# A hybrid decoder step on one core: the recurrence's products on the whole array, and the causal mask set by GpSimd selections

## The chip, the cores and the metric

The kernel runs on one core of one Trainium2 chip. A core has TensorE (PE in the profile; its weight loads are shown apart as PEld), VectorE (DVE), ScalarE (ACT), GpSimd (POOL) and SyncE (SP), which issues nearly all DMAs here. The engines work side by side, each through its own queue in a fixed order, and wait for one another by semaphores. The metric is the device time of one execution in microseconds (us). The time before is the median of three runs, 2099.18 us (2098.11 to 2101.88). A measurement of this kernel can tell a difference of about 0.2% from none.

## What is computed

One decoder layer with two groups of heads. From a prompt of 2048 positions and 64 sample positions, RMSNorm and one input projection give both groups; their gated outputs go through one output projection, a residual and a last norm. Group A is stick-breaking attention, causal over 2048 keys; group B is a matrix recurrence (RWKV-7), which the kernel works in chunks of 64 positions.

```python
def _sb_attend(q, k, v, q_pos, k_pos, sb_bias):
    z = jnp.einsum('bqhd,bkhd->bhqk', q, k) * (HEAD_DIM ** -0.5)
    z = z + sb_bias[None, :, None, None]
    mask = (k_pos[None, :] < q_pos[:, None])[None, None]
    log_keep = jnp.where(mask, jax.nn.log_sigmoid(-z), 0.0)
    between = lax.cumsum(log_keep, axis=3, reverse=True) - log_keep
    a = jnp.where(mask, jnp.exp(jax.nn.log_sigmoid(z) + between), 0.0)
    return jnp.einsum('bhqk,bkhd->bqhd', a, v)

def step(S, inp):                      # _wkv_scan, one position
    r_t, w_t, k_t, v_t, a_t, b_t = inp
    sa = jnp.einsum('bhvk,bhk->bhv', S, a_t)
    S = S * w_t[:, :, None, :] + sa[..., None] * b_t[:, :, None, :] + v_t[..., None] * k_t[:, :, None, :]
    return S, jnp.einsum('bhvk,bhk->bhv', S, r_t)
```

## The kernel before

**Planned order.** Every operation is first recorded (`Plan.op`) with an engine, a cost, what it reads and writes, and a priority. `Plan.issue` then lays them out by a list schedule: each engine takes the ready operation of lowest priority number, and the instructions are emitted in that order, which the chip keeps. TensorE's costs carry a mode: R for products on the whole 128x128 array, T for transposes, A, B, C and E for products on a part of it. `SWITCH` adds a cost when the mode changes. Because all operations are emitted through one helper, the profile gives nearly all of them the line L63; tiles tell them apart, and their buffer numbers are left out there.

**Stage 1 (proj).** The prompt goes in four quarters of 512 positions (`ORDER`, one string for each). `project` multiplies the normed input (`xh`, `xl`: high and low part) by the weights (`wp`): 4056 products of 128x512 or smaller. They have the last priority of all (1e6), so they fill whatever PE time the rest leaves. `rw_unit` handles two heads of the recurrence for one quarter: there are 16 units. `attend` handles two heads of attention for one block of 512 queries.

**A step of the recurrence (`seq`).** A unit has 8 chunks, worked one after another, so 128 steps in all. Each step has four groups of products. `fx` multiplies `L` by `VV` (in the trace `bank<-VV,L`); `fu` multiplies the inverse `NN` by `XT` (`bank<-XT,NN`); `fs` gives the new state from `BKT` and `VV` (`bank<-VV,BKT`); `fy` gives the output (`bank<-L,VV`, `bank<-AR,SZ`, `bank<-RS,VV`). Between them DVE and ACT copy the results from the banks. In `fx`, `fs` and `fy` the two heads use 64 columns of the array each, and `fu` uses 64 columns; so all four are column-tiled (mode A), where the projections use all 128 columns. A product of two f32 operands is two MATMULs in the trace, the xh and wp products (fp32r) are one.

**A chain of attention (`softmax_chain`).** For 128 queries of one head and up to 512 keys: two products of `kt` and `qt` into a bank; ACT computes |z| into `T` and relu(z) into `D`, then exp and ln on `T`; DVE scans `T` and `D` along the keys, then forms z minus the scan into `T`; PE transposes `T` (up to four 128x128); ACT takes the exponential into `At`; PE multiplies `At` by `vt` for two heads at a time (64 columns each). Of 320 such chains 128 are diagonal: their last 128 keys are those of the queries themselves. There a third product, `neg` by `idb` in bf16, adds -30000 where the key is not before the query. There are two `T` and two `D` buffers (more for the last `attend`) and two banks for scores (`ZB`), so two chains are under way at a time. GpSimd copies the carry (`car`) from one key block to the next, and serves the recurrence (`SW`, `SZ`).

**Stage 2.** After the last projection the remaining chains run, with the samples' attention and the output products (`woh`, `wol` by `orw`) beside them; the output products of the last quarter come after the last chain.

Of the kernel before, what the change touches and what calls it, by code (L numbers as in the profile page):

```python
# [79 lines left out]
class Plan:  # L80
# [67 lines left out]
    SWITCH = {("T", "T"): 81.0}  # L148
    for _a in "RT":
        for _b, _x, _y in (("A", 97.0, 55.0), ("B", 97.0, 50.0), ("C", 97.0, 90.0), ("E", 97.0, 15.0)):  # L150
            SWITCH[_a, _b] = _x + 75.0 * (_a == "T")
            SWITCH[_b, _a] = _y
    for _a in "ABCE":
        for _b in "ABCE":
            if _a != _b:
                SWITCH[_a, _b] = 75.0

# [185 lines left out]
class Kern:  # L343
# [146 lines left out]
    def stage1(self, ctx):  # L490
# [36 lines left out]
        self.consts2a()  # L527
# [17 lines left out]
    def consts1(self, S):  # L545
# [29 lines left out]
        bo, mask, mask8 = self.bo, self.mask, self.mask8  # L575
# [20 lines left out]
        op("POOL", 9500, masks, (), ["C1"])  # L596
        op("DVE", 130, lambda: nc.vector.tensor_copy(self.bor, bo), ["C1"], ["C1"])
# [9 lines left out]
        op("DVE", 210, lambda: nc.vector.tensor_copy(shT, bs.t[:, 0:136].rearrange("p (c b) -> p c b", b=8)), [bs.k], ["C1"])  # L607
# [5 lines left out]
    def const_tiles(self, S):  # L613
        nc = self.nc
        for nm, n in (("vt", 64), ("omu", 17), ("oka", 4), ("gneps", 1), ("bo", 128), ("mask", 128), ("mask8", 128), ("pv", 17), ("seqm", 8), ("sbb", 8)):
# [18 lines left out]

        self.d_w = self.tc.dram_tile([33, 2, 128, 1024], F32, name="d_w")
        self.d_x = self.tc.dram_tile([T, 1024], F32, name="d_x")
        self.d_g = self.tc.dram_tile([512, T], F32, name="d_g")

        self.d_o = self.tc.dram_tile([2, 1024, T], F32, name="d_o")

    def attention_tiles(self, S):
# [5 lines left out]
        self.neg = S.tile([128, 128], BF16, "neg")  # L647
        self.idb = S.tile([128, 128], BF16, "idb")
# [178 lines left out]
    def evac_rw(self, hf, ti, t0, Np, Ns, c0, ct, kind, j, bk):  # L827
# [17 lines left out]
        if Np < N:  # L845
# [3 lines left out]
            self.stt(vs[:, :, 0], self.shT[:, ct, :], mu, vs[:, :, 0], ALU.mult, ALU.add, r=[], w=zk, prio=-1)  # L849
# [16 lines left out]
    def rwkv_tiles(self, S):  # L866
# [34 lines left out]
        self.SZ = S.ring(2, [128, 64], F32, "SZ")  # L901
# [246 lines left out]
    def seq(self, hf, j, c, un):  # L1148
# [37 lines left out]
        self.act(xt.t[hi, 1], bx.t[hi, 0:64], AF.Copy, r=[bx.k], w=[(xt.k, 1)], ps=True, prio=-0.5)  # L1186
        bu = self.bank("XB")
        self.pe(224, lambda: self.mm(bu.t[lo, 0:128], un.NN[:, c, :], xt.t.rearrange("p h x -> p (h x)"), True, True), r=nks + [(xt.k, 0), (xt.k, 1)], w=[bu.k], prio=-0.5, mode="A")
        self.copy(VV[lo, s_, 1, 0, :], bu.t[lo, 0:64], r=[bu.k], w=[ku + (0,)], prio=-0.5)
        self.act(VV[lo, s_, 1, 1, :], bu.t[lo, 64:128], AF.Copy, r=[bu.k], w=[ku + (1,)], ps=True, prio=-0.5)  # L1190
        kus = [ku + (0,), ku + (1,)]
        bs = self.bank("XB")
        def fs():
            for h in range(2):
                self.mm(bs.t[hr[h], 0:64], BKT[:, s_, h, :], VV[:, s_, 1, h, :], True, True)
        self.pe(215, fs, r=[kb, kv] + kus, w=[bs.k], prio=-0.5, mode="A")
        last = c == 7
# [4 lines left out]
        if c == 0:
            self.yb = self.bank("YB")
        yb = self.yb
        y0 = 64 * c
        def fy():
            for h in range(2):
                self.mm(yb.t[hr[h], y0:y0 + 64], VV[:, s_, 1, h, :], un.L[h][:, c, 64:128], True, False)
            for h in range(2):
                st, rt = (VV[:, s_, 0, 1, :], un.RS[:, c, :]) if h else (sz.t, un.AR[:, c, 64:128])  # L1210
                self.mm(yb.t[hr[h], y0:y0 + 64], st, rt, False, True)
        self.pe(330, fy, r=kus + [kv, ks, sz.k, ("AR", U, c), ("RS", U)] + lks, w=[yb.k], mode="A")
# [301 lines left out]
    def consts2a(self):  # L1514
        nc = self.nc
        idt = self.ident.t
        neg, idb = self.neg.t, self.idb.t
        def f():
            nc.gpsimd.tensor_copy(idb, idt)

            nc.gpsimd.memset(neg, 0.0)
            nc.gpsimd.affine_select(out=neg, in_=neg, pattern=[[-1, 128]], base=-1, channel_multiplier=1, compare_op=ALU.is_ge, fill=-30000.0)
        self.pool(7800, f, w=["idb", "neg"])

# [51 lines left out]
    def softmax_chain(self, zb, n, bias, bk, car, first, last, rings):  # L1576
# [8 lines left out]
        self.act(t, t, AF.Ln, r=[T.k], w=[T.k], bias=1.0, tab=LNE)  # L1585
        init = 0.0 if first else car[0]
# [9 lines left out]
        self.stt(t, z, bias, d, ALU.add, ALU.subtract, r=[zb.k, D.k], w=[T.k])  # L1596
        return T

    def attend(self, t, j):
# [18 lines left out]
        for kb in range(t, -1, -1):  # L1618
# [6 lines left out]
            for qs in qss:  # L1625
# [3 lines left out]
                for h in range(2):  # L1629
# [6 lines left out]
                    D = self.softmax_chain(zb, n, self.sbb[:, 2 * j + h:2 * j + h + 1], [], (self.car.t[:, c:c + 1], (self.car.k, c)), diag, kb == 0, (self.Tr, self.Dr))  # L1636
# [215 lines left out]
```

## Time and profile before

| | us |
|---|---|
| median of three runs | 2099.18 |
| the profiled execution | 2096.49 |
| its span, first to last instruction | 2094.8 |
| PE busy | 1993.0 (95%), 15130 MATMULs |
| PEld busy | 1497.9 (72%) |
| DVE busy | 1607.3 (77%) |
| ACT busy | 1483.3 (71%) |
| POOL busy | 313.9 (15%), 854 instructions |
| DMA | 380.85 MB, 182 GB/s |

TensorE's clock was granted at 0.986 of its full 2.4 GHz over the span. A matmul's end is modelled and matmuls overlap, so PE's busy share says that something was always under way, not what each product cost. What a group of products costs is read from the starts of the products around it.

### The profile page before, as it was taken

The numbers are of one execution on the slowest core, as the hardware profiler recorded it, in microseconds if no ns is written. First come the engines' busy times: TensorE is split into PE (matmuls) and PEld (weight loads), VectorE is DVE, ScalarE is ACT, GpSimd is POOL, SyncE is SP. The second block draws the span as 40 slices with busy tenths as digits, with TensorE's granted clock in tenths as the row PEclk, the third lists the DMA queues.
The fourth block names the chain that finished last, engine by engine and source line by source line (L and its number), as shares of the span: only waits on it lengthen the run. The fifth ranks groups of instructions, "written<-read, shape, count | busy, mean of one in ns | idle before, by whom it ended". The sixth has DMA issues, their size and how long they took to land. (4 is left out here: it accounts for less than half of the span.)

```text
span 2094.8 us, 43112 instructions
## 1 busy us (share of the span) xinstructions
PE 1993.0 (95%) x15130; PEld 1497.9 (72%) x15130; DVE 1607.3 (77%) x3770; ACT 1483.3 (71%) x3115; POOL 313.9 (15%) x854
## 2 busy tenths in 40 slices
PE   6889999999999999999999999999997999999988
PEld 5787887767777777777677777767675767676645
DVE  7798698665887888788888989889866767676732
ACT  6555454586768787877777876777687888898831
POOL 4122222110012112111221121121112000000000
PEclk9899999999999999999999999999998999999999
DMA  6977746747775675666456555555665656656454
GB/s 232 330 250 213 221 131 196 199 144 238 206 217 148 196 194 150 173 193 179 136 162 184 153 145 145 177 146 159 185 165 160 209 174 187 190 168 178 142 163 132
DMA packets 346551, 380.85 MB, mean 182 GB/s; under 512 B 127923, under 2 KB 247273, under 8 KB 346333
## 3 DMA queue, kind: packets, MB, share of 16 engines
q1 hardware_dynamic: 345948, 378.00, 61.4%
q8 instruction: 119, 1.95, 0.4%
q14 instruction: 100, 0.81, 0.1%
q0 software_dynamic: 384, 0.10, 0.0%
HBM read 268.94 MB, written 102.76 MB: 177 GB/s over the span
## 5 line engine op out<-in xcount | busy, mean ns | idle before, releaser
L63 PE MATMUL bank<-xh,wp 128*128 128x512 f32 (+2 forms) x2704 | 785.5, 364 | 10.6 <-ACT wp L63 5.8
L63 PEld LDWEIGHTS bank<-xh,wp 128*128 128x128 f32 x2704 | 476.7, 190 | 88.4 <-issue 17.5
L63 PE MATMUL bank<-xl,wp 128*128 128x512 f32 (+2 forms) x1352 | 491.4, 364 | 0.0
L63 ACT ACTIVATE T<-T 128x512 f32<-128x512 f32 (+3 forms) x608 | 345.6, 569 | 6.0
L63 DVE TENSOR_TENSOR_SCAN D<-T,car,D 128x512 f32<-128x512 f32 x180 | 230.6, 1282 | 70.0 <-ACT T L63 65.2
L63 PEld LDWEIGHTS bank<-xl,wp 128*128 128x128 f32 x1352 | 257.4, 190 | 37.2 <-issue 8.1
L63 ACT ACTIVATE At<-bank 128x512 f32<-128x512 f32 (+3 forms) x304 | 161.2, 530 | 99.6 <-PE bank L63 96.3
L63 PE MATMUL bank<-kt,qt 128*128 128x512 f32 (+3 forms) x640 | 215.9, 411 | 1.8 <-issue 1.5
L63 DVE SCALAR_TENSOR_TENSOR T<-bank,sbb,D 128x512 f32<-128x512 f32 (+3 forms) x304 | 200.9, 661 | 6.8 <-PE bank L63 0.5
L63 ACT ACTIVATE T<-bank,sbb 128x512 f32<-128x512 f32 (+3 forms) x304 | 188.5, 620 | 21.2 <-PE bank L63 14.3
L63 ACT ACTIVATE D<-bank,sbb 128x512 f32<-128x512 f32 (+3 forms) x304 | 189.4, 624 | 14.7 <-DVE T L63 10.2
L63 PE MATMUL bank<-woh,orw 128*128 128x512 f32 (+1 forms) x544 | 184.2, 406 | 8.7 <-DMA orw<-d_o 8.6
L63 PE MATMUL bank<-ident,T 128*128 128x128 f32 (+1 forms) x1156 | 174.6, 274 | 9.4 <-DVE T L63 8.2
L63 DVE TENSOR_TENSOR IMP<-IMP,IA 128x2 f32<-128x2 f32 (+30 forms) x496 | 168.3, 339 | 18.3 <-POOL IA L63 10.8
L63 PEld LDWEIGHTS bank<-ident,T 128*128 128x128 f32 (+1 forms) x1156 | 124.8, 141 | 55.3 <-DVE T L63 20.3
L63 POOL TENSOR_TENSOR SW<-VV,WC 64x64 f32<-64x64 f32 x256 | 93.1, 366 | 395.2 <-DVE VV L63 358.5
L63 PE MATMUL bank<-At,vt 128*64 128x128 f32 x1992 | 143.9, 281 | 1.6 <-ACT At L63 0.9
L63 POOL COPY car<-D 128x1 f32<-128x1 f32 x180 | 45.5, 253 | 666.9 <-DVE D L63 606.0
L63 PEld LDWEIGHTS bank<-At,vt 128*64 128x64 f32 x1992 | 108.1, 137 | 41.4 <-issue 31.9
L63 DVE TENSOR_TENSOR_SCAN D<-T,D 128x128 f32<-128x128 f32 (+3 forms) x124 | 101.0, 814 | 46.9 <-ACT T L63 40.7
L63 PEld LDWEIGHTS bank<-woh,orw 128*128 128x128 f32 (+1 forms) x544 | 99.2, 186 | 41.0 <-issue 18.8
L63 DVE TENSOR_REDUCE IMP<-IMP 128x1 f32<-128x2 f32 (+30 forms) x496 | 121.2, 244 | 7.4
(330 smaller groups left out, 3417.2 us busy)
## 6 DMA issues: line engine op xcount, KB each, us to landing
wp<-d_w SPq DMA_DIRECT2D x198, 512.0 KB
d_w<-wp SPq DMA_DIRECT2D x66, 512.0 KB
kt<-d_k SPq DMA_DIRECT2D x80, 256.0 KB
wraw<-in_w_in SPq DMA_DIRECT2D x66, 256.0 KB
qt<-d_q SPq DMA_DIRECT2D x128, 128.0 KB
orw<-d_o SPq DMA_DIRECT2D x64, 256.0 KB
vt<-out_v_prompt SPq DMA_DIRECT2D x38, 256.0 KB
IA<-d_ia SPq DMA_DIRECT2D x64, 128.0 KB
```

Of the source, the lines that this page charges most:

```text
L63: return f(*[x.real() if isinstance(x, Lz) else x for x in a], **{k: x.real() if isinstance(x, Lz) else x for k, x in kw.items()})
```

## The change

**The recurrence.** `fx` now takes 66 columns of `L` (the two beyond 64 are not used) and puts the second head's result beside the first's, in columns 64 to 127 of the bank. `fu` takes two neighbouring chunks of `NN` as 128 columns, of which one half is used. `fs` is one product of both heads by both heads, 128x128, of which the diagonal blocks are used. So these three are products on the whole array (mode R). `fy` is taken out of the step into `rw_y`: four chunks' `fy` are issued together after every fourth chunk, still column-tiled. `SZ` has five buffers instead of two to keep the states until then.

**The mask.** `neg`, `idb` and their product are gone. In a diagonal chain GpSimd selects on the last 128 columns three times (`hide`): on `D` after the relu, on `T` after the ln, both with fill 0 ahead of the scan, and on `T` again with -30000 after the scan's use, ahead of the transposes. The selection keeps a column whose number is at most the row's.

**Planner and memory.** `SWITCH` has other numbers (97 into a tiled mode, 200 out of it, 150 between two, none between transposes), a group of n transposes is costed 109n + 2 instead of 109n - 66. `bo` shares memory with `bor`, `shT` with `shp`.

```diff
-    SWITCH = {("T", "T"): 81.0}
+    SWITCH = {}
     for _a in "RT":
-        for _b, _x, _y in (("A", 97.0, 55.0), ("B", 97.0, 50.0), ("C", 97.0, 90.0), ("E", 97.0, 15.0)):
-            SWITCH[_a, _b] = _x + 75.0 * (_a == "T")
-            SWITCH[_b, _a] = _y
+        for _b in "ABCE":
+            SWITCH[_a, _b], SWITCH[_b, _a] = 97.0, 200.0
...
-        self.pe(109 * len(terms) - 66, f, r=r, w=w, prio=prio, mode="T")
+        self.pe(109 * len(terms) + 2, f, r=r, w=w, prio=prio, mode="T")
...
-        self.SZ = S.ring(2, [128, 64], F32, "SZ")
+        self.SZ = S.ring(5, [128, 64], F32, "SZ")
...
-                self.mm(bx.t[hr[h], 0:64], un.L[h][:, c, 0:64], VV[:, s_, 0, h, :], True, True)
-        self.pe(215, fx, r=lks + [ks, kv], w=[bx.k], prio=-0.5, mode="A")
+                self.mm(bx.t[0:66, 64 * h:64 * h + 64], un.L[h][:, c, 0:66], VV[:, s_, 0, h, :], True, True)
+        self.pe(230, fx, r=lks + [ks, kv], w=[bx.k], prio=-0.5)
...
-        self.pe(224, lambda: self.mm(bu.t[lo, 0:128], un.NN[:, c, :], xt.t.rearrange("p h x -> p (h x)"), True, True), r=nks + [(xt.k, 0), (xt.k, 1)], w=[bu.k], prio=-0.5, mode="A")
+        c2, ur = min(c, 6), hr[c == 7]
+        self.pe(228, lambda: self.mm(bu.t[:, 0:128], un.NN[:, c2:c2 + 2, :].rearrange("p c i -> p (c i)"), xt.t.rearrange("p h x -> p (h x)"), True, True),
+                r=nks + [(xt.k, 0), (xt.k, 1)], w=[bu.k], prio=-0.5)
...
-        def fs():
-            for h in range(2):
-                self.mm(bs.t[hr[h], 0:64], BKT[:, s_, h, :], VV[:, s_, 1, h, :], True, True)
-        self.pe(215, fs, r=[kb, kv] + kus, w=[bs.k], prio=-0.5, mode="A")
+        self.pe(228, lambda: self.mm(bs.t[:, 0:128], BKT[:, s_].rearrange("p h x -> p (h x)"), VV[:, s_, 1].rearrange("p h x -> p (h x)"), True, True),
+                r=[kb, kv] + kus, w=[bs.k], prio=-0.5)
...
+        if c % 4 == 0:
+            self.late_y = []
+        self.late_y.append((c, s_, sz, kus + [kv, ks, sz.k, ("AR", U, c), ("RS", U)] + lks))
+        if c % 4 == 3:
+            self.rw_y(un, yb)
...
-        self.pe(330, fy, r=kus + [kv, ks, sz.k, ("AR", U, c), ("RS", U)] + lks, w=[yb.k], mode="A")
+    def rw_y(self, un, yb):
+        VV, hr = self.VV, self.HR
+        def fy(group=self.late_y):
+            for c, s_, sz, _ in group:
...
+        self.pe(962, fy, r=[k for g in self.late_y for k in g[3]], w=[yb.k], mode="A")
...
+    def hide(self, x, k, fill):
+        self.pool(300, lambda: self.nc.gpsimd.affine_select(out=x, in_=x, pattern=[[-1, 128]], base=0, channel_multiplier=1, compare_op=ALU.is_ge, fill=fill), w=[k])
...
+        if hide:
+            self.hide(d[:, n - 128:n], D.k, 0.0)
+            self.hide(t[:, n - 128:n], T.k, 0.0)
...
+        if hide:
+            self.hide(t[:, n - 128:n], T.k, -30000.0)
...
-                    self.products([(zb.t[:, 0:n], x, K.t[:, h, 0:n], []) for x in qq] + [(zb.t[:, n - 128:n], self.idb.t, self.neg.t, [])] * diag,
-                                  [(q.k, qs // 2, 0), (q.k, qs // 2, 1), (K.k, 0), (K.k, 1), "idb", "neg"], [zb.k])
+                    self.products([(zb.t[:, 0:n], x, K.t[:, h, 0:n], []) for x in qq],
+                                  [(q.k, qs // 2, 0), (q.k, qs // 2, 1), (K.k, 0), (K.k, 1)], [zb.k])
```

The planner works the whole order out anew, so no engine keeps its order. Three places follow in which it matters. In the rows names are as in the trace with buffer numbers, `x2` counts repeats, and the last item is rows by columns of what is written (64x64: 64 columns of the array are used).

PE inside a unit in the third quarter, before: `fs` and `fy` of one step, projections, `fx` of the next.

```order
L63 MATMUL bank_6_69<-kt_143,qt_145 128x512
L63 MATMUL bank_7_70<-VV_111,BKT_110 64x64 x2
L63 MATMUL bank_3_66<-L_15_89,VV_111 64x64
L63 MATMUL bank_3_66<-L_16_90,VV_111 64x64
L63 MATMUL bank_3_66<-AR_87,SZ_116 64x64
L63 MATMUL bank_3_66<-RS_93,VV_111 64x64
L63 MATMUL bank_6_69<-kt_143,qt_145 128x512
L63 MATMUL bank_1_64<-xh_191,wp_197 128x512
L63 MATMUL bank_1_64<-xl_192,wp_197 128x512
L63 MATMUL bank_1_64<-xh_191,wp_197 128x512
L63 MATMUL bank_1_64<-xh_191,wp_198 128x512
L63 MATMUL bank_4_67<-VV_111,L_15_89 64x64
```

PE inside a unit in the third quarter now: `fu`, `fs`, and then the first of four chunks of `fy`.

```order
L63 MATMUL bank_8_71<-xh_193,wp_200 128x512
L63 MATMUL bank_7_70<-XT_114,NN_91 128x128
L63 MATMUL bank_8_71<-xl_194,wp_200 128x512
L63 MATMUL bank_8_71<-xh_193,wp_200 128x512 x2
L63 MATMUL bank_8_71<-xl_194,wp_200 128x512
L63 MATMUL bank_8_71<-xh_193,wp_200 128x512
L63 MATMUL bank_5_68<-ident_80,T_154 128x128 x4
L63 MATMUL bank_6_69<-VV_111,BKT_110 128x128
L63 MATMUL bank_4_67<-L_15_89,VV_111 64x64
L63 MATMUL bank_4_67<-L_16_90,VV_111 64x64
L63 MATMUL bank_4_67<-AR_87,SZ_119 64x64
L63 MATMUL bank_4_67<-RS_93,VV_111 64x64
```

`fx`, `fu` and `fs` now stand among products of the same width, and only `fy` leaves it. A stretch of PE's order in which only 64 columns or fewer are written occurs 648 times before and 343 times now; up to the last projection it is 505 times and 187 times.

POOL in the second quarter, before: the recurrence's copies and the carries.

```order
L63 MEMSET IA_123 128x32
L63 TENSOR_TENSOR SW_122<-VV_111,WC_96 64x64 x2
L63 COPY SZ_117<-VV_111 64x64
L63 TENSOR_TENSOR SW_121<-VV_111,WC_96 64x64 x2
L63 COPY SZ_116<-VV_111 64x64 x2
```

POOL in the second quarter now: selections (`AFFINE_SELECT`) on `T` and `D` stand between them.

```order
L63 AFFINE_SELECT T_154<-T_154 128x128
L63 COPY car_183<-D_156 128x1
L63 AFFINE_SELECT T_154<-T_154 128x128
L63 TENSOR_TENSOR SW_128<-VV_111,WC_106 64x64 x2
L63 COPY SZ_118<-VV_111 64x64
L63 TENSOR_TENSOR SW_127<-VV_111,WC_96 64x64 x2
L63 COPY SZ_119<-VV_111 64x64
L63 AFFINE_SELECT D_156<-D_156 128x128
L63 AFFINE_SELECT T_154<-T_154 128x128
L63 COPY car_183<-D_156 128x1
```

384 selections come into a queue that served no chain but for its carry.

PE at the end of the projections, before: the last of them, and the recurrence's last step.

```order
L63 MATMUL bank_5_68<-RS_103,VV_111 64x64
L63 MATMUL bank_6_69<-xl_192,wp_198 128x512
L63 MATMUL bank_6_69<-xh_191,wp_198 128x512
L63 MATMUL bank_8_71<-VV_111,L_23_99 64x64
L63 MATMUL bank_8_71<-VV_111,L_24_100 64x64
L63 MATMUL bank_2_65<-ident_80,ev_201 128x128 x4
L63 MATMUL bank_1_64<-XT_114,NN_101 64x128
```

PE at the end of the projections now: after the last of them the last unit's inverse (`SPT`) still comes, and its eight steps behind it.

```order
L63 MATMUL bank_2_65<-xh_193,wp_200 128x512
L63 MATMUL bank_2_65<-xl_194,wp_200 128x512
L63 MATMUL bank_2_65<-xh_193,wp_200 128x512 x2
L63 MATMUL bank_2_65<-xl_194,wp_200 128x512
L63 MATMUL bank_2_65<-xh_193,wp_200 128x512
L63 MATMUL bank_1_64<-SPT_112,L_23_99 32x32
L63 MATMUL bank_1_64<-SPT_112,L_24_100 32x32
```

Ahead of the last projection there stood 211 chains' products (104 of them diagonal) and 127 of the 128 steps; now there stand 197 chains' and 120 steps.

## Rows read from the trace of the kernel before

**Rows 1.** Windows: length, busy us (count) per engine, clock, DMA share, GB/s.

```profile
390.00:1576.00 1186.00, 1159.24 (x8761) 861.52 (x8760) 970.50 (x2308) 903.66 (x1884) 182.37 (x531) 1.00 0.61 174
1576.00:1997.00 421.00, 402.57 (x3010) 282.55 (x3009) 293.46 (x423) 356.86 (x712) 26.38 (x101) 0.97 0.60 179
```

**Rows 2.** Tile xh: count, ns min/median/max, first and last start in us.

```profile
L63 PE MATMUL bank<-xh,wp x2704: 274/389/792, 16.5 to 1576.1; 128*128 128x512 f32 x110, 128*128 128x256 f32 x49, 128*128 128x320 f32 x35
```

**Rows 3.** Timeline of PE, fs with fy, then fx: start us, length, tiles, count.

```profile
1088.99 0.39 PE L63 MATMUL bank<-xh,wp 128*128 128x512 f32 x1
1089.31 0.34 PE L63 MATMUL bank<-VV,BKT 128*64 128x64 f32 x4
...
1089.81 0.50 PE L63 MATMUL bank<-xh,wp 128*128 128x512 f32 x1
1090.15 0.39 PE L63 MATMUL bank<-xl,wp 128*128 128x512 f32 x1
1090.38 0.40 PE L63 MATMUL bank<-xh,wp 128*128 128x512 f32 x1
1090.71 0.34 PE L63 MATMUL bank<-VV,L 128*64 128x64 f32 x4
1090.97 0.50 PE L63 MATMUL bank<-xh,wp 128*128 128x512 f32 x1
1091.31 0.39 PE L63 MATMUL bank<-xl,wp 128*128 128x512 f32 x1
```

**Rows 4.** Timeline of PE around one fu.

```profile
454.02 0.39 PE L63 MATMUL bank<-xl,wp 128*128 128x512 f32 x1
454.34 0.43 PE L63 MATMUL bank<-XT,NN 128*64 128x128 f32 x2
454.71 0.73 PE L63 MATMUL bank<-xh,wp 128*128 128x512 f32 x2
455.28 0.40 PE L63 MATMUL bank<-xl,wp 128*128 128x512 f32 x1
```

**Rows 5.** Timeline of PE: an f32 product on the whole array (splitr by bo).

```profile
252.57 0.28 PE L63 MATMUL bank<-xh,wp 128*128 128x256 f32 x1
252.69 0.33 PE L63 MATMUL bank<-splitr,bo 128*128 128x64 f32 x2
252.83 0.37 PE L63 MATMUL bank<-xh,wp 128*128 128x256 f32 x1
253.03 0.28 PE L63 MATMUL bank<-xl,wp 128*128 128x256 f32 x1
```

**Rows 6.** Page, costliest groups: weight loads of 128 and of 64 columns.

```profile
L63 PEld LDWEIGHTS bank<-xh,wp 128*128 128x128 f32 x2704 | 476.7, 190 | 88.4 <-issue 17.5
L63 PEld LDWEIGHTS bank<-At,vt 128*64 128x64 f32 x1992 | 108.1, 137 | 41.4 <-issue 31.9
```

**Rows 7.** Timeline of PE: three transposes, a diagonal chain's products, its mask product.

```profile
464.11 0.39 PE L63 MATMUL bank<-xl,wp 128*128 128x512 f32 x1
464.34 0.49 PE L63 MATMUL bank<-ident,T 128*128 128x128 f32 x3
464.59 0.71 PE L63 MATMUL bank<-kt,qt 128*128 128x512 f32 x2
465.14 0.23 PE L63 MATMUL bank<-neg,idb 128*128 128x128 bf16 x1
465.18 0.71 PE L63 MATMUL bank<-xh,wp 128*128 128x512 f32 x2
465.73 0.39 PE L63 MATMUL bank<-xl,wp 128*128 128x512 f32 x1
```

**Rows 8.** Groups on POOL: busy us, mean ns; selections of 128x128.

```profile
L63 POOL TENSOR_SCALAR_AFFINE_SELECT neg<-neg 128x128 bf16<-128x128 bf16 x1 | 0.5, 486 | 0.1
L63 POOL TENSOR_SCALAR_AFFINE_SELECT ident<-ident 128x128 f32<-128x128 f32 x1 | 0.3, 293 | 0.1
```

**Rows 9.** Tile car: ns min/median/max of the carry's copy on POOL.

```profile
L63 POOL COPY car<-D x180: 178/186/1093, 494.4 to 1963.9; 128x1 f32<-128x1 f32 x180
```

More of the change, by code (lines that the diff above doesn't have):

```diff
@@ L155 @@
             if _a != _b:
-                SWITCH[_a, _b] = 75.0
+                SWITCH[_a, _b] = 150.0
     def clock(self, s, cost, share):
@@ L526, in stage1 @@
         self.nat = 0
-        self.consts2a()
         for hf in range(4):
@@ L573, in consts1 @@
                ["vt"], ["C0"])
-        bo, mask, mask8 = self.bo, self.mask, self.mask8
+        bo, mask, mask8 = self.W3.t[:, 0:128], self.mask, self.mask8
         def masks():
@@ L595, in masks @@
                                                     compare_op=ALU.is_ge, fill=0.0)
-        op("POOL", 9500, masks, (), ["C1"])
-        op("DVE", 130, lambda: nc.vector.tensor_copy(self.bor, bo), ["C1"], ["C1"])
+        op("POOL", 9500, masks, (), ["C1", self.W3.k])
+        op("DVE", 130, lambda: nc.vector.tensor_copy(self.bor, bo), ["C1", self.W3.k], ["C1"])
         shT = self.shT
@@ L606, in consts1 @@
             op("PE", 107 * n, tr, keys, [bs.k])
-        op("DVE", 210, lambda: nc.vector.tensor_copy(shT, bs.t[:, 0:136].rearrange("p (c b) -> p c b", b=8)), [bs.k], ["C1"])
+        op("DVE", 210, lambda: nc.vector.tensor_copy(shT, bs.t[:, 0:136].rearrange("p (c b) -> p c b", b=8)), [bs.k], ["C1"] + [("shp", c) for c in range(17)])
         seqm, sbb = self.seqm, self.sbb
@@ L614, in const_tiles @@
         nc = self.nc
-        for nm, n in (("vt", 64), ("omu", 17), ("oka", 4), ("gneps", 1), ("bo", 128), ("mask", 128), ("mask8", 128), ("pv", 17), ("seqm", 8), ("sbb", 8)):
+        for nm, n in (("vt", 64), ("omu", 17), ("oka", 4), ("gneps", 1), ("mask", 128), ("mask8", 128), ("pv", 17), ("seqm", 8), ("sbb", 8)):
             setattr(self, nm, S.tile([128, n], F32, nm).t)
@@ L618, in const_tiles @@
         self.bor = S.tile([128, 128], F32R, "bor").t
-        self.shT = S.tile([128, 17, 8], F32, "shT").t
+        self.bo = self.bor.bitcast(F32)
         self.shp = S.tile([128, 17, 9], F32, "shp").t
+        self.shT = self.shp[:, :, 0:8]
         self.rm = S.tile([128, 512], BF16, "rm").t
@@ L848, in evac_rw @@
             self.stt(vs[:, :, 1:8], pp[:, :, 0:7], mu, vs[:, :, 1:8], ALU.mult, ALU.add, r=[bk.k], w=zk, prio=-1)
-            self.stt(vs[:, :, 0], self.shT[:, ct, :], mu, vs[:, :, 0], ALU.mult, ALU.add, r=[], w=zk, prio=-1)
+            self.stt(vs[:, :, 0], self.shT[:, ct, :], mu, vs[:, :, 0], ALU.mult, ALU.add, r=[shk], w=zk, prio=-1)
             self.copy(self.shp[:, ct, 0:8], pp[:, :, 7], r=[bk.k], w=[shk], prio=-1)
@@ L1199, in seq @@
             out = self.SP[:, j, h] if last else VV[lo, sn, 0, h, :]
-            self.stt(out, bs.t[hr[h], 0:64], un.WN[hr[h], c:c + 1], sw.t[hr[h]], ALU.mult, ALU.add,
+            self.stt(out, bs.t[hr[h], 64 * h:64 * h + 64], un.WN[hr[h], c:c + 1], sw.t[hr[h]], ALU.mult, ALU.add,
                      r=[bs.k, (sw.k, h), ("WN", U)], w=[("SP", j)] if last else [("VVS", sn)], prio=-0.5)
[L1202 to L1211, printed above, removed]
-        self.pe(330, fy, r=kus + [kv, ks, sz.k, ("AR", U, c), ("RS", U)] + lks, w=[yb.k], mode="A")
+    def rw_y(self, un, yb):
+        VV, hr = self.VV, self.HR
+        def fy(group=self.late_y):
+            for c, s_, sz, _ in group:
+                for h in range(2):
+                    self.mm(yb.t[hr[h], 64 * c:64 * c + 64], VV[:, s_, 1, h, :], un.L[h][:, c, 64:128], True, False)
+                for h in range(2):
+                    st, rt = (VV[:, s_, 0, 1, :], un.RS[:, c, :]) if h else (sz.t, un.AR[:, c, 64:128])
+                    self.mm(yb.t[hr[h], 64 * c:64 * c + 64], st, rt, False, True)
+        self.pe(962, fy, r=[k for g in self.late_y for k in g[3]], w=[yb.k], mode="A")
     def rw_out(self, hf, j, t0, N, c0, un, yb):
@@ L1512, in stage2 @@
         self.P.issue(lambda t: nc.scalar.preload_act_table_set(t))
[L1514 to L1523, printed above, removed]
     def consts2b(self):
@@ L1574, in load_wout, with softmax_chain @@
                 self.tt(l, x.t, h.bitcast(F32), ALU.subtract, r=[x.k, ("woh", k, c)], w=[("wol", k, c)])
-    def softmax_chain(self, zb, n, bias, bk, car, first, last, rings):
+    def hide(self, x, k, fill):
+        self.pool(300, lambda: self.nc.gpsimd.affine_select(out=x, in_=x, pattern=[[-1, 128]], base=0, channel_multiplier=1, compare_op=ALU.is_ge, fill=fill), w=[k])
+    def softmax_chain(self, zb, n, bias, bk, car, first, last, rings, hide=False):
         nc = self.nc
@@ L1632, in attend @@
                     qq = [q.t[:, qs // 2, c:c + 128] for c in (128 * (qs % 2), 256 + 128 * (qs % 2))]
[L1633 to L1634 removed]
+                    self.products([(zb.t[:, 0:n], x, K.t[:, h, 0:n], []) for x in qq],
+                                  [(q.k, qs // 2, 0), (q.k, qs // 2, 1), (K.k, 0), (K.k, 1)], [zb.k])
                     c = 4 * h + qs
[L1636 removed]
+                    D = self.softmax_chain(zb, n, self.sbb[:, 2 * j + h:2 * j + h + 1], [], (self.car.t[:, c:c + 1], (self.car.k, c)), diag, kb == 0, (self.Tr, self.Dr), diag)
                     tb = self.bank("TB")
```

11 lines of the change are left out of this document (6 added, 5 removed).

## The prediction

> **What bounds the kernel now.** I read first the windows of the trace, cut at the last projection. It starts at 1576.1 us [rows 2]. Before it, from 390 us on, PE is busy for 1159 of 1186 us (98%), DVE for 970 (82%), ACT for 904 (76%) and POOL for 182 (15%) [rows 1]: PE is the bound, because projections fill whatever the rest leaves. In this stretch and the 390 us ahead of it 211 chains and 127 steps are done. Behind it, to 1997 us, PE is still called busy for 403 of 421 us, but there is no filler any more, and ACT is at 357 (85%) [rows 1]. 109 chains end there, one in 421/109 = 3.86 us. I take that stretch as paced by the chains (ACT and its hand-overs), since a long busy share of PE there is also a matmul that waits. From 1997 us to the end stand the last output products, which the change leaves alone.
>
> PE's busy time does not price a product. I price a group by the starts of the projections around it: a 512-column fp32r product follows the one before in 0.23 us where nothing lies between (1090.15 to 1090.38 [rows 3]), and a 256-column one in 0.12. What is over is the group's.
>
> - `fs` and `fy`: 1088.99 to 1090.15 less two products, 0.70. `fx`: 1090.38 to 1091.31 less two, 0.47 [rows 3]. The time ahead of a group holds two products in both cases.
> - The two pairs of `fy` are thus 0.70 - 0.47 = 0.23, and one pair 0.115. `fx` is one pair, so going into a column-tiled stretch and out of it costs 0.47 - 0.115 = 0.355.
> - `fu`: 454.02 to 455.28 less three, 0.57 [rows 4], so 0.21 without the 0.355.
> - An f32 product on the whole array, two passes: 252.57 to 253.03 less two of 0.12, 0.22 [rows 5], and no 0.355. One pass is 0.11.
>
> The Trainium skill (TensorEngine Tiling (Array Packing), Key Properties) says that a change of the tiling mode drains TensorE. The 0.355 of [rows 3] agrees.
>
> **The recurrence.** Streaming: before, a step had `fx` 0.115, `fu` 0.21, `fs` 0.115, `fy` 0.23, together 0.67. After, `fu` and `fs` are each one f32 product on the whole array, 0.22. `fx` is now four passes one after the other. Their price is not in the trace: at the 0.11 of [rows 5] they are 0.44; if a pass of 64 columns follows as fast as its weights are loaded (a load of 64 columns takes 137 ns, of 128 columns 190 [rows 6]), about 0.24. I take 0.24, since `fx` streams 64 columns and loads 66, and keep 0.44, which is 128 x 0.20 = 26 us more. `fy` stays at 0.23. A step then streams 0.24 + 0.22 + 0.22 + 0.23 = 0.91.
>
> Up to the last projection 505 tiled stretches become 187: 318 x 0.355 = -113 us. Streaming: 120 steps at 0.91 less 127 at 0.67 = +24 us. For the whole program it is 305 x 0.355 = -108 and 128 x 0.24 = +31.
>
> The late `fy` has nobody waiting but the unit's output, which needs all eight chunks anyway, and the copy into `SZ`, which has five buffers for four chunks: 0, and if POOL did stop there, the next `SW` behind it would hold the state, a part of the waits below. The number of copies on DVE and ACT is unchanged. The second head's `XT` and the last chunk's `fu` are read from other rows or columns of the bank, and cost the same. Merged memory (`bo`, `shT`) and constants that go are start-up work on POOL and cost nothing.
>
> **The mask on PE.** Three transposes with one mask product: 464.11 to 465.73 less five products, 0.47 [rows 7]. A transpose is one pass of 128 columns, 0.11 by [rows 5], so the mask product is 0.47 - 0.33 = 0.14 (0.135 unrounded). 104 of them stand ahead of the last projection: -14 us; 128 in all: -17.
>
> **The moved chains.** 197 chains instead of 211 stand ahead of the last projection. One streams two products (0.46), four transposes (0.44) and its products with `vt`, for which no row stands alone and which I take as much as the transposes, 0.44: 14 x 1.34 = -19 us of PE ahead, and 14 chains more behind, at 3.86 each: +54.
>
> **The selections.** 384 on POOL. The rows of like shape are 293 ns in f32 and 486 ns in bf16 [rows 8]: 112 to 187 us, on an engine that is 85% idle, so their busy time costs nothing. Their latency may. `D` is selected while ACT does exp and ln on `T`, so it is hidden; the two on `T` stand in the chain, ahead of the scan and ahead of the transposes. Two at 0.29 to 0.49 add 0.6 to 1.0 us to a diagonal chain. What stands behind them: the scan in DVE's queue, and behind that the recurrence's copies; the transposes in PE's queue, and behind those the projections. PE's order is fixed, so a late transpose stops the filler too.
>
> How much of it reaches PE is the term that the trace cannot give. Lower bound 0: two chains are under way, and the planner can put filler ahead of each transpose. Upper bound: two parts. First, the chains keep their pace of 1186/211 = 5.62 us, and 197 of them then need 1107 us where 1186 - 122 = 1064 are left: 43. Second, every diagonal chain passes on half of 1.0 us (two chains are under way), 104 x 0.5 = 52. Together 95. I take 30, in the lower half, since DVE, the next engine, goes from 82% to some 88% in the shorter stretch and is still short of full [rows 1], and chains behind the projections show that 3.86 us is possible.
>
> **The sum**, on the profiled execution of 2096.5 us. PE up to the last projection: -113 + 24 - 14 - 19 = -122. Chains behind it: +54. New waits: +30. Together -38: the last projection starts at about 1576 - 122 + 30 = 1484 us, and the end is 2058.5. The median is 2.7 above the profiled execution: **2061 us**. With `fx` at 0.44 it is 2061 + 26 = 2087.
>
> **The rivals.**
>
> A. PE's saving reaches the end in full: no new waits, and the chains behind the projections aren't paced by ACT. Then PE's whole -108 + 31 - 17 = -94 is the gain: 2005. For it: PE at 96% behind the projections, too [rows 1]. Against: ACT at 85% there. Region 2005 to 2030.
>
> B. The chains set the pace (slower). Selections and the held cadence cost 95 instead of 30: -122 + 54 + 95 = +27, 2126. It decides once the new waits are over 122 - 54 = 68 us, that is 0.35 us for each of 197 chains. For it: fixed orders, DVE at 82%, two `T` buffers, and a select ahead of a scan that makes DVE wait with the state's update behind it. Against: chains are 3.86 us apart where nothing else is in the way. Region 2103 to 2135.
>
> C. No change: waits of 64 to 72 us meet the saving, or 40 with `fx` at 0.44. A difference under 0.2%, 4 us, can't be measured here.
>
> D. Selections stand behind DVE's work. The carry's copy on POOL takes 178 ns at best, 186 in the median, but 1093 at worst [rows 9]. If each of the two selects took the worst case, a diagonal chain would pass on 1.09 instead of 0.5: 104 x 1.09 = 113, the waits were 156 and the time 2187. The median speaks against it: most copies aren't held. The Trainium skill (SBUF — State Buffer, SBUF: two separate sides) states such an exclusive lock between VectorE and GpSimd, under which the loser waits for a whole instruction; by it D is the case, and the worst of [rows 9] agrees, the median doesn't.
>
> E. The tiled stretches weren't dear, and what is read as 0.355 goes to others. Then only streaming (+31) and the mask (-17) remain: 2113. [Rows 3, 5] speak against it. The Trainium skill (TensorEngine Tiling (Array Packing), Theoretical Speedup) states up to twice the rate for dimensions of 64 or less; it speaks against this change, as two heads side by side are given up, and the +31 is what the rows make of it.
>
> **How the numbers follow.** The forecast's own case, 2030 to 2092, with waits between 0 and 60: 0.58. A 0.14, C 0.07, B 0.15, D 0.03, E 0.03. Faster by over 0.2% are the first two: 0.72. Within 0.2% is C: 0.07. Slower are B, D and E: 0.21. The range is 2012 to 2118: it leaves out about a third of A, half of B and D, 0.15 together, and it reaches over both ends of `fx`'s price and of the waits but for the worst.
>
> **What the profile after would show.** If the steps are right: `fx`, `fu` and `fs` between projections cost 0.22 to 0.24 over them; the last projection starts near 1484 us (1454 without new waits, 1549 at B's); PE's idle share ahead of it rises from 2% to 4 or 5%, with waits on POOL or DVE named; selections take 0.3 to 0.5 us; chains behind the last projection stay near 3.9 us apart. If it starts near 1454 and chains behind follow faster than 3.86, A is right. If DVE waits for POOL ahead of scans and PE for `T`, B; if selections have a mean near 1 us, D; if a step on the whole array still costs over 0.4 us for `fu` or `fs`, E. I am wrong in the sum if the tiled stretches' price falls elsewhere, as where the 0.355 was in part a wait for the banks.

## The result and the profile after

The changed kernel takes 2070.45 us (median of four, 2063.81 to 2075.45) where the kernel before took 2098.64 beside it: a ratio of 0.9862, 95% interval 0.9835 to 0.9889. It is 28 us faster; 2061 was forecast. The profiled execution took 2069.06 us.

Busy time by engine, then the two windows that answer to [rows 1] (columns as there), then the tile `xh` as in [rows 2]:

```profile
PE 1955.5 (95%) x14746; PEld 1518.0 (73%) x14746; DVE 1612.8 (78%) x3770; ACT 1484.3 (72%) x3115; POOL 447.2 (22%) x1238
```

```profile
390.00:1512.00 1122.00, 1085.84 (x7895) 845.23 (x7896) 934.63 (x2236) 855.17 (x1774) 272.92 (x796) 0.99 0.63 177
1512.00:1970.00 458.00, 436.02 (x3335) 304.72 (x3335) 323.51 (x471) 397.69 (x798) 65.79 (x218) 0.97 0.56 166
```

```profile
L63 PE MATMUL bank<-xh,wp x2704: 274/389/735, 15.2 to 1512.1; 128*128 128x512 f32 x110, 128*128 128x256 f32 x46, 128*128 128x320 f32 x38
```

The last projection starts at 1512.1 us, 64 us earlier than before (1484 was forecast). Behind it 123 chains take 458 us, 3.72 each (475 forecast). The tail is 98 us, as it was. 64 us less ahead and 37 more behind make the 27 us between the two profiled executions.

One step inside the program, on PE (start, length, tiles, count):

```profile
624.23 0.39 PE L63 MATMUL bank<-xl,wp 128*128 128x512 f32 x1
624.46 0.40 PE L63 MATMUL bank<-VV,L 128*66 128x64 f32 x4
624.66 0.71 PE L63 MATMUL bank<-xh,wp 128*128 128x512 f32 x2
625.21 0.39 PE L63 MATMUL bank<-xl,wp 128*128 128x512 f32 x1
625.44 0.61 PE L63 MATMUL bank<-xh,wp 128*128 128x512 f32 x2
626.02 0.49 PE L63 MATMUL bank<-XT,NN 128*128 128x128 f32 x2
626.26 0.48 PE L63 MATMUL bank<-xl,wp 128*128 128x512 f32 x1
626.58 0.62 PE L63 MATMUL bank<-xh,wp 128*128 128x512 f32 x2
627.04 0.40 PE L63 MATMUL bank<-xl,wp 128*128 128x512 f32 x1
627.28 0.62 PE L63 MATMUL bank<-xh,wp 128*128 128x512 f32 x2
627.74 0.38 PE L63 MATMUL bank<-VV,BKT 128*128 128x128 f32 x2
627.87 0.47 PE L63 MATMUL bank<-xl,wp 128*128 128x512 f32 x1
628.19 0.39 PE L63 MATMUL bank<-xh,wp 128*128 128x512 f32 x1
```

Priced as in the prediction: `fx` 624.23 to 625.21 less three products, 0.29. `fs` 627.28 to 628.19 less three, 0.22. `fu` 625.44 to 626.58 less three, 0.45. So `fs` has the price of [rows 5] here and `fu` has twice that. Waits account for the difference. A wait is most often shown at the weight load, PEld, while PE is still called busy with the product before it. PEld's waits of the changed kernel, and then of the kernel before (in all, times, longest):

```profile
PEld bank L63 <- ACT XT L63: 37.2, 81, 2.2
PEld bank L63 <- ACT VV L63: 36.1, 80, 1.9
PEld bank L63 <- DVE T L63: 24.1, 52, 4.9
...
PEld bank L63 <- POOL T L63: 6.9, 15, 1.0
...
PEld bank L63 <- DVE VV L63: 3.3, 10, 0.5
```

```profile
PEld bank L63 <- ACT XT L63: 27.4, 72, 0.8
PEld bank L63 <- DVE T L63: 24.5, 51, 2.7
PEld bank L63 <- DVE VV L63: 18.7, 54, 1.3
...
PEld bank L63 <- ACT VV L63: 10.0, 28, 0.9
```

The waits that grew most are the recurrence's own: `fu` waits for ACT's copy into `XT`, `fs` for ACT's copy into `VV`, 73 us together where it was 37. The waits for DVE's writes into `VV`, most of them ahead of `fx`, went down from 18.7 to 3.3, so all three together grew from 56 to 77. These sums are rough. Idle time of PEld ahead of a column-tiled group is not all a wait for the operand named, as this load of `fs` in the kernel before shows: its operand had been copied 0.29 us earlier (experiment 5), and `fs` does not read `IMP`.

```profile
1089.31 0.20 PEld L63 LDWEIGHTS bank<-VV,BKT 128*64 128x64 f32 x4 [0.35 <-DVE IMP L63]
```

The prices of the steps, in the next section, tell the waits more cleanly. The transposes wait for DVE's `T` as long as before; 6.9 us stand under the selections themselves (`POOL T`), which is new. The selections themselves, by form (busy us, mean ns), the tile `car` as in [rows 9], and what DVE's scans wait for:

```profile
L63 POOL TENSOR_SCALAR_AFFINE_SELECT T<-T 128x128 f32<-128x128 f32 x248 | 90.0, 365 | 215.9 <-ACT T L63 100.9 <-DVE T L63 95.8 <-DVE VV L63 3.6
L63 POOL TENSOR_SCALAR_AFFINE_SELECT D<-D 128x128 f32<-128x128 f32 x124 | 42.6, 343 | 224.9 <-ACT D L63 207.5 <-PE bank L63 12.5 <-ACT VV L63 3.0
```

```profile
L63 POOL COPY car<-D x180: 173/183/1578, 472.2 to 1939.5; 128x1 f32<-128x1 f32 x180
```

```profile
DVE D L63 <- ACT T L63: 71.9, 69, 4.3
DVE D L63 <- POOL T L63: 54.1, 51, 3.1
```

### The profile page after: what moved, and what is told of

Read it like the earlier page. It is cut to its first block, busy times and chain, and to the rows that moved or that the text cites. A ratio compares the mean times of both kernels' runs of the same rounds, so it can differ in the third digit from the quotient of the medians.

```text
span 2067.4 us, 43009 instructions
## 1 busy us (share of the span) xinstructions
PE 1955.5 (95%) x14746; PEld 1518.0 (73%) x14746; DVE 1612.8 (78%) x3770; ACT 1484.3 (72%) x3115; POOL 447.2 (22%) x1238
## 4 chain that ended last, share of the span: by engine, by line
PE 47%; DVE 17%; ACT 12%; DMA 6%; issue 3%; POOL 1%; SPq 1%; DVEq 0%; POOLq 0%; ACTq 0%
PE bank L63 47%; DVE IMP L63 5%; ACT T L63 4%; DVE D L63 3%; DVE T L63 2%; DVE VV L63 1%; ACT D L63 1%; DMA IMP<-d_im 1%; ACT VV L63 1%; SPq L63 1%; ACT At L63 1%; ACT tmprn L63 1%; DVE xl L63 1%; POOL T L63 1%; ACT ev L63 1%
## 5 line engine op out<-in xcount | busy, mean ns | idle before, releaser
L63 PE MATMUL bank<-kt,qt 128*128 128x512 f32 (+3 forms) x640 | 210.8, 403 | 0.7 <-issue 0.6
L63 PE MATMUL bank<-woh,orw 128*128 128x512 f32 (+1 forms) x544 | 190.5, 412 | 1.3 <-DMA orw<-d_o 1.3
L63 DVE TENSOR_TENSOR_SCAN D<-T,D 128x128 f32<-128x128 f32 (+3 forms) x124 | 102.7, 828 | 59.2 <-POOL T L63 54.1
L63 POOL TENSOR_SCALAR_AFFINE_SELECT T<-T 128x128 f32<-128x128 f32 x248 | 90.0, 365 | 215.9 <-ACT T L63 100.9
```

What stands on the lines that cost most here:

```text
L63: return f(*[x.real() if isinstance(x, Lz) else x for x in a], **{k: x.real() if isinstance(x, Lz) else x for k, x in kw.items()})
```

## How the experiments are read

**Two kinds of run.** In some kernels the planner works the order out anew (e1 to e8). In others the order of before or after is kept, group for group, and only what a group issues is changed (e9 to e12). The second kind takes the order out of the comparison.

**The price of a step.** Where a group stands alone between products of the projections, the scores or the output, its price is the start behind it less the start ahead, less those products' own 0.23 us (0.12 for 256 columns), waits included. The means over all such places, in ns, with the number of places:

| kernel | fx | fu | fs | fs with fy | a step, us |
|---|---|---|---|---|---|
| before | 548 (47) | 630 (45) | | 765 (42) | 1.94 |
| e9 | 337 (47) | 439 (45) | | 1063 (42) | 1.84 |
| e5 | 396 (51) | 464 (48) | | 980 (37) | 1.84 |
| e10 | 477 (45) | 613 (56) | 527 (40) | 1458 (14) | 1.85 |
| changed | 326 (45) | 490 (56) | 451 (40) | 1678 (14) | 1.57 |
| e3 | 380 (51) | 373 (53) | 363 (43) | 1532 (14) | 1.41 |

Where four `fy` go together, a step is `fx` + `fu` + three quarters of `fs` + a quarter of `fs` with `fy`: 0.326 + 0.490 + 0.338 + 0.420 = 1.57. A step's price does not by itself set the time: e9, e5 and e10 have the same to 0.01 us and take 2094, 2096 and 2080 us, and e3, which has the shortest step, is 20 us slower than the changed kernel.

Theory 1 says that the shorter products are waited away at `fu` and `fs`; theory 2 that the selections are the new wait; theory 3 that one order against another weighs as much as the products.

## Experiment 1: the mask alone, and its undoing

e1 puts the selections into the kernel before; e2 puts the product back into the changed kernel. In both the order is new.

```diff
-self.products([...] + [(zb.t[:, n - 128:n], self.idb.t, self.neg.t, [])] * diag, ...)
+self.products([...], ...)
...
+if hide:
+    self.hide(t[:, n - 128:n], T.k, -30000.0)
```

> The kernel before with the selections on GpSimd in place of the mask product, and nothing else of the change; the planner lays out anew, and 201 chains instead of 211 stand ahead of the last projection. Theory 1 (the new waits of the changed kernel stand at fu and fs, not at the selections): PE loses 104 mask products of 0.135 ahead of the last projection, -14 us, and 10 chains go behind it, where they cost 3.72 instead of some 1.34 of PE, +24: 2095 to 2110 us. Theory 2 (the selections' latency is the new wait, 30 us or more): 2125 us or more, and scans that wait for POOL with PE idle behind them.

> The changed kernel with the mask product back and no selections. 204 chains instead of 197 ahead of the last projection. Theory 1: PE gains 14 us of products, 7 chains fewer behind give back 17: 2060 to 2080 us, and fu and fs still start within 60 ns of their copies' end in most steps. Theory 2: the waits go with the selections: 2030 to 2050 us.

e1 took 2120.15 us, ratio 1.0109 (1.0074 to 1.0144): slower than before by 22 us. e2 took 2073.41, ratio 0.9891 (0.9857 to 0.9925), which overlaps the changed kernel's 0.9862. So the recurrence with its tables gives the gain, and the mask nothing that these runs can tell. Theory 2 falls with e2, which was to be at 2050 or less. But e1 is 10 us beyond what theory 1 allows, and its last projection explains little: it starts only 10 us earlier than before, and the 119 chains behind it and the tail take 34 us more.

```profile
L63 PE MATMUL bank<-xh,wp x2704: 274/389/796, 16.9 to 1566.4; 128*128 128x512 f32 x110, 128*128 128x256 f32 x43, 128*128 128x320 f32 x41
```

## Experiment 2: the waits at fu and fs

> The changed kernel with the four copies of a step between fx, fu and fs (two on DVE, two on ACT) priced in the planner at what the trace shows, 212 and 216 ns, instead of 132 and 103; no instruction is added or removed. 185 chains instead of 197 ahead of the last projection. Theory 1: fu and fs come later in PE's order, their mean cost between two projections falls from 0.49 and 0.43 us to under 0.35, -30 to -45 us ahead of the last projection; 12 chains more behind, +29: 2050 to 2070 us. Theory 2: fu and fs cost the same as in the changed kernel, and only the chains count: 2085 to 2100 us.

```diff
-self.copy(xt.t[lo, 0], bx.t[lo, 0:64], r=[bx.k], w=[(xt.k, 0)], prio=-0.5)
+self.copy(xt.t[lo, 0], bx.t[lo, 0:64], r=[bx.k], w=[(xt.k, 0)], prio=-0.5, cost=212)
...
-self.act(xt.t[hi, 1], ..., prio=-0.5)
+self.act(xt.t[hi, 1], ..., prio=-0.5, cost=216)
```

PEld's waits of e3, and its last projection:

```profile
PEld bank L63 <- ACT XT L63: 21.1, 43, 2.1
...
PEld bank L63 <- ACT VV L63: 18.4, 41, 2.7
...
PEld bank L63 <- DVE VV L63: 14.0, 27, 3.0
```

```profile
L63 PE MATMUL bank<-xh,wp x2704: 274/389/795, 15.2 to 1495.0; 128*128 128x512 f32 x110, 128*128 128x256 f32 x46, 128*128 128x320 f32 x38
```

The waits for ACT's copies went as theory 1 says, from 73 to 40 us (with DVE's writes into `VV`, from 77 to 54), and the means of `fu` and `fs` from 0.49 and 0.45 to 0.37 and 0.36. The last projection starts 17 us earlier. But the kernel takes 2090.24 us, ratio 0.9942 (0.9910 to 0.9974), slower than the changed one: 135 chains instead of 123 stand behind the last projection, and what comes behind it takes 607 us of the span instead of 555. The waits are real, and taking them out by a new order gave more away than it won. The time lies in theory 2's range, whose mechanism (an unchanged `fu`) is wrong. (The profiled execution is the slowest of e3's, 14 us over its median, and that is in the 607.)

## Experiment 3: what an order is worth

> The kernel before with only the planner's new numbers (mode changes and transposes). No instruction differs, the order does: 241 chains instead of 211 stand ahead of the last projection. If where the chains stand is worth what the windows say (3.86 us behind, 1.34 us of PE ahead), 30 chains give 30 x 2.5 = 76 us: 2020 to 2035 us. If the chains ahead only move the last projection by as much as they save behind it: 2090 to 2105 us, with the last projection at 1640 to 1690 us.

> The changed kernel with 5 ns more for each group of products with vt in the planner's costs. No instruction differs; the order is worked out anew, with 201 chains instead of 197 ahead of the last projection. Theory 3 (one order against another is worth as much as the whole change): 2070 us plus or minus 15 or more. Otherwise within 8 us of 2070.

> The kernel before with the same 5 ns: 225 chains instead of 211 ahead of the last projection, no instruction differs. Theory 3: 2098 us plus or minus 15 or more, and the last projection moves with the chains. Otherwise within 8 us of 2098.

```diff
-self.pe(218 * nk + 55, fo, ...)
+self.pe(218 * nk + 60, fo, ...)
```

(The diff is that of e7 and e8; e4 has the tables shown in the change.) Last projections of e4 and e8:

```profile
L63 PE MATMUL bank<-xh,wp x2704: 274/389/792, 15.2 to 1695.8; 128*128 128x512 f32 x110, 128*128 128x256 f32 x47, 128*128 128x320 f32 x37
```

```profile
L63 PE MATMUL bank<-xh,wp x2704: 274/389/795, 16.7 to 1618.9; 128*128 128x512 f32 x110, 128*128 128x256 f32 x49, 128*128 128x320 f32 x35
```

e8, which differs from the kernel before in nothing but an order worked out from 5 ns more in one cost, takes 2118.00 us, ratio 1.0108 (1.0057 to 1.0159). The same 5 ns in the changed kernel give 2061.87, 0.9835 (0.9782 to 0.9887), which overlaps the 0.9862. Theory 3 holds for the kernel before: its order was a good one, and a neutral step loses 20 us. e4 takes 2145.89, 1.0231 (1.0180 to 1.0282): the new tables alone, on the old products, cost 48 us.

They also price a moved chain. In e4 30 more chains ahead of the last projection start it 120 us later and take 69 us off what comes behind it; in e8 14 more cost 43 and take 23 off. So a chain ahead cost 4.0 and 3.1 us there, not the 1.34 of PE that I took, and one behind gave 2.3 and 1.7, not 3.86. With e3 and e1, where 12 and 10 chains went behind and the time there grew by 52 and 34 us, no single price fits.

## Experiment 4: fy in its step, and no mask at all

> The changed kernel with fy issued in each step again, instead of four chunks' together; fx, fu and fs stay on the whole array, the selections stay. 90 more column-tiled stretches ahead of the last projection than in the changed kernel. If each stretch costs the 0.355 of the prediction: 90 x 0.355 = 32 us, less 4 chains fewer behind: 2090 to 2105 us. If a stretch costs little in the running kernel (Theory 1 has it that the time saved on switches is waited away at fu and fs): 2065 to 2080 us.

```diff
-        if c % 4 == 0:
-            self.late_y = []
+        self.late_y = []
...
-        if c % 4 == 3:
-            self.rw_y(un, yb)
+        self.rw_y(un, yb)
...
-        self.pe(962, fy, ...)
+        self.pe(242, fy, ...)
```

e5 takes 2095.97 us, ratio 0.9995 (0.9974 to 1.0016): the whole gain is gone. That is what the stretches' price gave, 2090 to 2105. The table says more: `fx` and `fu` cost about what they do in the changed kernel, but `fs` with one `fy` costs 0.98, and a step 1.84 where it was 1.94 before. The order is another one here, so up to some 20 us of it can be the order's.

> The changed kernel without any causal mask in the diagonal chains: neither selections nor the product; this leaves a part of the computation out. Against the changed kernel it tells what the selections cost, against the one with the product back what the product costs. Theory 1: the product's 17 us of PE is its price (some 2055 us here against 2073), and the selections cost about as much, 15 us, by their latency. Theory 2 (the selections are the new wait, 30 us or more): 2040 us or less.

e6 takes 2066.58 us, ratio 0.9867 (0.9822 to 0.9911), the changed kernel's own. Neither theory's number came: the selections cost nothing that shows when the order is free to change with them.

## Experiment 5: one thing changed in a kept order

> The kernel before in its own order, instruction group for instruction group, with fx, fu and fs on the whole array; the planner's costs are left as they were, fy stays in its step, the mask product stays. By the prices between projections fx gains 0.47 - 0.296, fu 0.565 - 0.23, and fs with fy goes from 0.70 to some 0.81, since fy still needs the tiled array: -0.40 for each of 128 steps, 51 us. Theory 1: part of it is waited away at fu and fs: 2045 to 2070 us. Theory 3 (the order decides, not the products): 2085 to 2100 us.

```diff
-self.mm(bx.t[hr[h], 0:64], un.L[h][:, c, 0:64], VV[:, s_, 0, h, :], True, True)
+self.mm(bx.t[0:66, 64 * h:64 * h + 64], un.L[h][:, c, 0:66], VV[:, s_, 0, h, :], True, True)
...
-            for h in range(2):
-                self.mm(bs.t[hr[h], 0:64], BKT[:, s_, h, :], VV[:, s_, 1, h, :], True, True)
+            self.mm(bs.t[:, 0:128], BKT[:, s_].rearrange("p h x -> p (h x)"), VV[:, s_, 1].rearrange("p h x -> p (h x)"), True, True)
```

e9 takes 2093.55 us, ratio 0.9972 (0.9958 to 0.9986): 6 us of the 51 that the prices promise. Its last projection, PEld's waits, and the step of [rows 3] in it (PE with PEld and ACT):

```profile
L63 PE MATMUL bank<-xh,wp x2704: 274/389/796, 16.5 to 1576.8; 128*128 128x512 f32 x110, 128*128 128x256 f32 x49, 128*128 128x320 f32 x35
```

```profile
PEld bank L63 <- ACT VV L63: 33.2, 81, 1.3
PEld bank L63 <- ACT XT L63: 24.8, 67, 0.8
```

```profile
1091.57 0.39 PE L63 MATMUL bank<-xh,wp 128*128 128x512 f32 x1
...
1091.68 0.21 ACT L63 ACTIVATE VV<-bank 64x64 f32<-64x64 f32 x1
...
1091.93 0.30 PEld L63 LDWEIGHTS bank<-VV,BKT 128*128 128x128 f32 x2 [0.41 <-ACT VV L63]
1091.94 0.49 PE L63 MATMUL bank<-VV,BKT 128*128 128x128 f32 x2
...
1092.36 0.34 PE L63 MATMUL bank<-L,VV 128*64 128x64 f32 x4
...
1092.74 0.50 PE L63 MATMUL bank<-xh,wp 128*128 128x512 f32 x1
...
1093.07 0.40 PE L63 MATMUL bank<-xl,wp 128*128 128x512 f32 x1
```

In the kernel before, at this step, ACT's copy into `VV` ran like this:

```profile
1088.81 0.21 ACT L63 ACTIVATE VV<-bank 64x64 f32<-64x64 f32 x1
```

There it ended at 1089.02, and `fs` started at 1089.31 [rows 3], 0.29 us later: no wait. In e9 it ends at 1091.89 and the weight load of `fs` starts at 1091.93, as soon as it can. `fx` and `fu` had become shorter, PE came to `fs` sooner, ACT did not, and `fs` with `fy` took 1091.57 to 1093.07 less two, 1.04 instead of 0.70. The last projection starts at the same time as before, to 0.7 us. The table has `fx` -0.21, `fu` -0.19, `fs` with `fy` +0.30, together -0.10 a step. Taken over all steps ahead of the last projection, from the start of the product ahead of a group to that of the one behind it, `fx` and `fu` take 34 us less and `fs` with `fy` 32 us more. Some 0.11 a step of that, 14 us, was expected, because `fy` alone still needs the column-tiled array; the other 18 go with the waits for ACT's copy into `VV`, 33.2 us where it was 10.0.

> The changed kernel in its own order with fx, fu and fs on 64 columns again; fy stays in groups of four, the selections stay. By the same prices fx loses 0.175 and fu 0.335 a step, and fs costs some 0.47 instead of 0.225: +0.75 for each of 128 steps, 96 us if PE pays it in full; Theory 1: the waits of some 40 us at fu and fs are no longer waited, so 2110 to 2135 us. Theory 3: 2070 to 2085 us.

e10 takes 2080.49 us, ratio 0.9914 (0.9896 to 0.9932). Against the changed kernel that is 0.9914 / 0.9862 = 1.0053 (plus or minus 0.0032 from the two intervals), some 11 us of the 96 that PE's prices ask, and less than theory 1's 2110; its last projection starts 20 us later, at 1532.3 us. It fits theory 3's range. `fu` again costs 0.56 where it does not wait, so the price of a tiled stretch is as it was read; what is lost on PE is for the most part not lost at the end.

> The changed kernel in its own order, without the 384 selections (they stay in the plan and are not issued); the mask is left out of the computation. Theory 1: their latency is hidden behind fixed orders in which PE waits elsewhere, 0 to -15 us: 2055 to 2070 us. Theory 2: -30 us or more: 2040 us or less.

> The kernel before in its own order, without the 128 mask products (they stay in the plan and are not issued); the mask is left out of the computation. By the prediction's price 128 x 0.135 = 17 us, 14 of it ahead of the last projection: 2080 to 2086 us. If PE only waits longer at the transposes that follow: 2093 to 2100 us.

The diffs are one line each: the selection, or the mask product, is planned and not issued.

```diff
-        self.pool(300, lambda: self.nc.gpsimd.affine_select(...), w=[k])
+        self.pool(300, lambda: None, w=[k])
```

e11 takes 2062.92 us, ratio 0.9824 (0.9802 to 0.9846): against the changed kernel 0.9961 (plus or minus 0.0035), so the selections cost between nearly nothing and 15 us, with 8 in the middle. e12 takes 2095.34, 0.9986 (0.9969 to 1.0003): the 128 products, with a mean price of 0.15 us each at 52 places of the kernel before, cost 3 us where 17 were taken, and perhaps nothing. DVE's scans in e11 wait almost only for ACT:

```profile
DVE D L63 <- ACT T L63: 108.8, 99, 4.1
```

With the selections it was 71.9 for ACT and 54.1 for POOL: 17 us more in all, not 104 times 0.5. Most of the time that a scan waits for the selection it would have waited for ACT.

## Why the prediction came out as it did

The time, 2061 forecast and 2070.45 measured, and the sign were right; of the steps behind them several were not, and the errors partly cancelled: the last projection came 64 us earlier where 92 were forecast, and what stands behind it took 37 us more where 54 were. That the time fits to 10 us is in part luck.

**PE as the bound.** This is the step that failed. I read 98% busy [rows 1] as "PE is the bound" and took each us of PE's work for a us of time, less one lump of new waits. Two runs with the order kept take work from PE and the end hardly moves (e9: 51 us of work, 6 at the end; e12: 17 and 3), and one adds it (e10: 96 and 11). A busy PE is often a PE whose next weight load stands waiting behind a product shown as under way. The Trainium skill (Perfetto Trace Analysis, Identifying the Most-Contended Engine) says that the matmul's busy share does not tell how close TensorE is to its limit, and names, beside the rate of arithmetic, the busy share of the weight loads; by [rows 1] that is 862 of 1186, 73%, and e9 and e12 agree with it.

**The prices.** The stretch's 0.355 was right where nothing waits: `fs` and `fu` on the whole array cost 0.22 to 0.23 when their operand was copied 0.15 us ahead or more, `fu` on 64 columns in e10 still 0.56. `fx` measured 0.296, between my 0.24 and 0.44: 7 us over 120 steps. Rival E is out, though by the prediction's own sign, over 0.4 us for `fu` or `fs`, it would hold: their means are 0.49 and 0.45. The sign did not part a dear stretch from a late operand.

**From price to step.** Taken without waits, a step should have gone from 0.47 + 0.57 + 0.70 = 1.74 to some 1.07: 0.30 + 0.23 + 0.22, and 0.32 as a quarter of a stretch with four `fy`. With waits it went from 1.94 to 1.57: 47 us over 128 steps instead of some 85. In 41 of 56 places `fu` starts within 0.06 us of the end of its copy and costs 0.57 on average.

**New waits.** I took 30 of 0 to 95, at the selections and the scans. By the prediction's own sum and the last projection they are 122 - 64 = 58 us. The size was inside the bounds; the place was for the most part wrong. The waits within a step grew from 1.94 - 1.74 = 0.20 to 1.57 - 1.07 = 0.50, some 38 us over 128 steps; the selections show with 6.9 at the transposes, and for what is left of the 58 no row stands alone. PE's idle share ahead of the last projection went from 2% to 3%, not to 4 or 5%, since most of the waiting lies under a product called busy. I had priced the step's copies only as unchanged, and had not asked whether they would now be late.

**The mask.** Both sides were too dear: the product 3 us, not 17; the selections some 8, with a mean of 0.36 and a median of 0.29 us, so rival D is out. What it fears does occur, but seldom: the worst took 1.69, and of 372 selections 16 began with 0.3 us or more of a scan on DVE still to run; 14 of these ended 0.08 to 0.09 us behind the scan's end. In the changed kernel the two cancel (e2, e6).

**Moved chains.** +54 was forecast behind the last projection, +37 came, and what the 14 chains were worth ahead of it can't be told apart. Experiment 3 shows why no fixed price holds: an order moved by a trifle shifts both sides by tens of us.

**Rivals.** B needed 68 us of new waits, 85 with the +37 that the chains gave; 58 came. Its sign, scans on DVE that wait for POOL, did show (54.1 us), but these waits stand for the most part in place of waits for ACT (experiment 5). A and C didn't occur.

**Where the 28 us came from.** With the order kept, the whole-array products are worth 6 us in the old order and 11 in the new one. The rest, some 17 to 22, goes with the order, in which the late `fy`, the tables and the free choices of the planner are mixed. That the late `fy` is its core is likely but not shown. For it: it alone of the parts, taken back, returns the kernel to 2096, and over all runs here the seven kernels with `fy` late (changed, e2, e3, e6, e7, e10, e11) take 2062 to 2090 us and the seven with `fy` in its step (before, e1, e4, e5, e8, e9, e12) 2094 to 2146, with column-tiled and with whole-array products on both sides. Against: e5 has an order of its own, and an order by itself is worth up to 20 us here; no run moves `fy` alone in the kernel before. What makes one order better stays open: the number of chains ahead of the last projection does not tell it (201 in e1 and e7, 2120 and 2062 us). No version with the mask in it beat the changed kernel beyond the intervals.

## What to carry to other kernels

Where an order is fixed, a product made shorter moves the end only if the operand of the next one comes sooner too: look for the weight load's wait and for the copy that ends just ahead of it before adding up PE's time. Before crediting a change that lets a planner lay out anew, run it once with the old order kept and run the old kernel once with a trifling change to its costs; here the second alone moved the time by 1%. Taking one kind of work out of a few hundred places, planned but not issued, gives its price in one run.

## What the runs showed of the hardware

In these kernels it is the weight load of an f32 product that stands for a late moving operand: in e9 the load of `fs` had 0.41 us of idle time ahead of it, until ACT's copy into `VV` was done, although the weights, `BKT`, had been copied last at 1087.4 us, 4 us earlier. At none of the 41 places where `fu` of the changed kernel follows its copy within 0.06 us does the load start ahead of the copy's end. In the trace the load itself carries the wait for the copy, so these runs do not tell whether the weights could be loaded ahead if only the product waited. A late operand thus costs the load as well: `fu` costs 0.23 us with 0.15 us or more between copy and start, 0.31 with 0.06 to 0.10, and at least 0.32 with less. The copies of 64x64 from a bank, which decide when that is, take 0.21 us on ACT, as at 1091.68 above.

A selection that meets a scan on DVE waits for it: the 14 named above took until 0.08 to 0.09 us behind the scan's end, where the median of all is 0.29 us.
